# A two-block network on one core: elementwise work of GpSimd moved to the vector engine up to the end of the expert loop

## The chip, the core and the metric

The kernel runs on one NeuronCore of a Trainium2 chip. Such a core has a matrix engine (PE in the profile, with its weight loads as PEld), a vector engine (DVE), a scalar engine (ACT), GpSimd (POOL) and SyncE (SP), which issues most of the DMAs. The metric is the device time of one launch in microseconds (us); lower is better. About 0.2% is what repeated timings of this kernel can tell from no change.

## The reference, cut to what matters

512 tokens of width 1024 pass through two blocks.

- First block. 16 meta tokens are put in front. A normalised input times `w_in` gives five parts: a gated convolution of 3 taps, and a gated convolution of 31 taps over 512 channels with a layer norm behind it. Their outputs, normalised, go through `w_out` into the residual. Then comes a layer of 16384 experts: for each token and each of 8 heads the 16 best experts out of 128 x 128 are chosen by two half-keys of 128 (`top_k` of 16 on either half, then `top_k` of 16 over the sums). An expert is one row of `u` and one row of `v`: the output is the sum over the chosen experts of `gelu(u . x) * gate * v`.
- Second block. A gated feed-forward layer of width 2816, two attention mixers with gates, and another such feed-forward layer.

All products must hold nearly float32 precision. The kernel therefore splits each matrix into a high part (a cast to fp32r) and a low part (the float32 value minus the high part) and adds three products: high x high, high x low, low x high.

## The kernel before, in words

**Weights.** `load_w` (line 79) takes a tile of 128 x 1024 float32 weights by DMA into `wf`, then `split` (line 89) casts it to the high part `wh` on the scalar engine (line 93) and subtracts to the low part `wl` (line 98). The low part is made on the vector engine by default and on GpSimd where the caller says `lo="p"`. `wf`, `wh` and `wl` have three buffers each, shared by all callers.

**Order.** Each engine works through its own queue in order. The Tile framework lays out these queues: it follows program order as a priority and its own timeline of when an instruction can start. A few instructions are kept in program order by hand (`keep_in_program_order`): the GpSimd gathers and the first product of each step of the pinned expert tiles.

**First block** (`block1`). 20 column tiles of `w_in` go through `proj` (line 198); their low parts are made on GpSimd, but for the first. `conv` (line 211) makes the 31 taps of one of four channel tiles: a tap is one multiply-add of 128 x 512 on the vector engine (line 221). For channel tile 0, 20 of its taps are instead a scalar-engine multiply (line 218) and a GpSimd addition (line 219). Twelve products with the norm's factor `rs` are on GpSimd too: `sg` (line 239), `xs` (line 274), `cv` (line 289), four each.

**Routing** (`peer`, lines 458 to 536). For each head two tiles of `peer_wq` are multiplied (low parts on GpSimd from head 1 on), scored against the half-keys, and the vector engine picks the best 16 by max, index and replace operations; candidates are built by small additions (line 487) and a GpSimd subtraction `dk` (line 507, which the change leaves alone) serves to read the chosen expert's number. In the shadow of this the matrix engine runs expert tiles 2 to 14 (`u_tile`, line 538), which come later in program order.

**Gate matrix** (lines 542 to 567). Three of the four token tiles go through all experts ("dense"); for them a matrix of gates by expert is needed. For each block of 8 tokens, one-hot rows of the first half-index (`o1`, line 556) and of the second (`oa`, line 557) are made by comparing `iota` with broadcast values, 128 x 1024 at once. `o1` times the gate gives `ob`: 5 of the 8 tokens on GpSimd (line 558), 3 on the scalar engine (line 560). 8 products `oa` x `ob` (line 564, two groups of four) are copied to `stg` by the scalar engine and sent to DRAM for each 16 tokens. Expert tiles 15 to 21 are spread as pinned steps among these blocks.

**Expert loop** (lines 569 to 635). In each of 128 iterations: the activations of a coming expert tile (`u_steps`, line 397: 24 products of 128 x 384, the low part of `u_t` on GpSimd), the gated activation `hf` (line 624) and its split, and 18 products of 128 x 512 with `peer_v` (low part on the vector engine; on GpSimd in the last 25 iterations, which have no `u` tile). The fourth token tile takes its experts by gathers instead: 256 indirect DMAs issued by GpSimd (lines 576 and 587), each followed by a multiply-add over 128 x 1024 on the vector engine (lines 579 and 590); four `row` buffers.

**Behind it** come the second block's feed-forward and attention, with some elementwise work on GpSimd that the change doesn't touch.

Of the kernel before, what the change touches and what calls it, by code (L numbers as in the profile page):

```python
# [27 lines left out]
# columns of the packed per-channel vectors, [128, NCONST]  # L28
# [17 lines left out]
class Ctx:  # L46
    def split_x(self, n=T):
        """The two parts of what the next products take, [128, 8, n]."""
        self.hh = self.xp.tile([P, KD, NM + T], F32R, tag="hh", name="hh", bufs=1)[:, :, 0:n]
        self.hl = self.xp.tile([P, KD, NM + T], F32R, tag="hl", name="hl", bufs=1)[:, :, 0:n]  # L50
        return self.hh, self.hl

    def split_tok(self):
        """The same, token tile by token tile: [128, 4, 8, 128]."""
        r = []
        for tag in ("hh", "hl"):
            t = self.xp.tile([P, KD, NM + T], F32R, tag=tag, name=tag, bufs=1)
            r.append(t.rearrange("p k n -> p (k n)")[:, 0:KD * T].rearrange("p (t k n) -> p t k n", t=4, k=KD))
        self.hh, self.hl = r
        return r  # L60

    def rows(self):
        """8 tiles [128, T], two to a buffer"""
# [15 lines left out]
def load_w(c, src, lo="v", hi="a", n=1024, p=P):  # L79
    """One weight unit [128, n]: the float32 values and their exact two-part split."""  # L80
# [20 lines left out]
def tok_ss(c, pool, tp, srcs, width):  # L101
    """PSUM [128, tiles]: sums of squares over the channels, token on the partitions.

    srcs: the channel tiles [128 channels, width]."""
# [15 lines left out]
def rsqrt(c, out, ss, n):  # L120
    """out = 1 / sqrt(ss / n + eps), a few columns; one Newton step on the table's square root

    Several n are those of as many parts of the columns."""
# [16 lines left out]
def col_rs(c, pool, tp, srcs, n, width, tag, bufs=1):  # L140
    """PSUM [128, width]: 1 / sqrt(mean over the n channels + eps) of each column, on every partition."""
# [16 lines left out]
def block1(c, A):  # L158
# [7 lines left out]
    with ExitStack() as es:  # L166
# [23 lines left out]
        # the products take the residual times the gain; the norm's factor of a token goes to what they give  # L190
# [7 lines left out]
        def proj(j, w=None):  # L198
            wh, wl = w or load_w(c, A["w_in"][j], lo="p")
# [11 lines left out]
        def conv(i, pool_taps=()):  # L211
            """A channel tile of the 31 taps, a step for each tap."""
            o = CONST_COLS["cf_w"][0] + 31 * i
            nc.scalar.activation(out=acc[i], in_=ub[:, i, 0:T], func=AF.Identity, scale=C[:, o:o + 1], bias=col("cf_b", i))
            for k in range(1, 31):
                if k in pool_taps:
                    t = tp.tile([P, T], F32, tag="tap", name="tap", bufs=2)
                    nc.scalar.mul(out=t, in_=ub[:, i, k:k + T], mul=C[:, o + k:o + k + 1])
                    nc.gpsimd.tensor_tensor(out=acc[i], in0=acc[i], in1=t, op=ALU.add)
                else:  # L220
                    nc.vector.scalar_tensor_tensor(out=acc[i], in0=ub[:, i, k:k + T], scalar=C[:, o + k:o + k + 1], in1=acc[i], op0=ALU.mult, op1=ALU.add)
# [12 lines left out]
        for i in range(4):  # L234
# [4 lines left out]
            nc.gpsimd.tensor_tensor(out=sg, in0=sg, in1=rs, op=ALU.mult)  # L239
# [3 lines left out]
            if i == 0:  # L243
                taps = conv(0, range(31 - c.ptaps, 31))
                some_taps(30 - c.ptaps)
# [4 lines left out]
        def gained(src, gname, i, k, l):  # L250
            """A channel tile times the gain, in two parts; its squares."""
# [18 lines left out]
        for i in range(4):  # L270
# [3 lines left out]
            nc.gpsimd.tensor_tensor(out=xs, in0=xs, in1=rs, op=ALU.mult)  # L274
# [14 lines left out]
            nc.gpsimd.tensor_tensor(out=cv, in0=cv, in1=rs[:, NM:], op=ALU.mult)  # L289
# [55 lines left out]
        # the next norm, token on the partitions; then features on the partitions, split  # L345
# [27 lines left out]
        # the first of the experts' tiles need the dense tokens only  # L373
# [8 lines left out]
GT = 3            # the token tile whose experts are gathered; the others go through all experts  # L382
ND = 3 * P        # tokens of the dense tiles
# [6 lines left out]
GRP = 8           # expert tiles whose gates are read at once  # L390
TG = 16           # tokens per block of the gate matrix


def u_steps(c, A, i, ps, alloc, pin=False):
    """The activations of 128 experts for the dense tokens, a step for each k-tile; pinned, a step stays behind
    what is before it on the tensor engine."""
    nc = c.nc
    wh, wl = load_w(c, A["u_t"][i], lo="p")
# [15 lines left out]
def peer(c, A):  # L414
# [9 lines left out]
    with ExitStack() as es:  # L424
# [26 lines left out]
        with tc.tile_pool(name="pr", bufs=1) as pr, tc.tile_pool(name="prp", bufs=2, space=PSUM) as pp:  # L451
# [6 lines left out]
            # routing, head by head  # L458
            mxs = []
            for h in range(NH):  # L460
                VI = pr.tile([P, 2, 2, 4, TOPK], F32, tag="VI", name="VI", bufs=2)
                ii = pr.tile([P, 2, 4, TOPK], U32, tag="ii", name="ii", bufs=2)
                for half in range(2):
                    wh, wl = load_w(c, A["peer_wq"][2 * h + half], lo="p" if h else "v")
# [36 lines left out]
                # the chosen experts: candidate j's key is j * 2^15 + expert - 2^14; less position * 2^15,  # L501
                # the chosen one's is the only one of an absolute value up to 2^14 that stands for an expert
# [8 lines left out]
            # gates: softmax over the chosen 16 of each head  # L511
# [10 lines left out]
            # the dense tiles' experts and gates, slot on the partitions  # L522
# [19 lines left out]
        with tc.tile_pool(name="pg", bufs=1) as pg, tc.tile_pool(name="pgp", bufs=2, space=PSUM) as pp:  # L542
            B, BP = 8, 5
            for tg in range(ND // TG):
                stg = pg.tile([P, NE, TG], F32, tag="stg", name="stg", bufs=2)
                for q in range(TG // B):
# [7 lines left out]
                    o1 = pg.tile([P, B, P], F32, tag="o1", name="o1", bufs=2)  # L554
                    ob = pg.tile([P, B, P], F32, tag="ob", name="ob", bufs=3)
                    nc.vector.tensor_tensor(out=o1, in0=ib, in1=both(0), op=ALU.is_equal)  # L556
                    nc.vector.tensor_tensor(out=oa, in0=ib, in1=both(1), op=ALU.is_equal)  # L557
                    nc.gpsimd.tensor_tensor(out=ob[:, 0:BP, :], in0=o1[:, 0:BP, :], in1=both(2)[:, 0:BP, :], op=ALU.mult)
                    for j in range(BP, B):
                        nc.scalar.activation(out=ob[:, j, :], in_=o1[:, j, :], func=AF.Copy, scale=sT[:, 2, t0 + j:t0 + j + 1])  # L560
# [10 lines left out]
        with tc.tile_pool(name="pd", bufs=1) as pd, tc.tile_pool(name="pv", bufs=1, space=PSUM) as pv:  # L571
# [33 lines left out]
            def gathers(spent):  # L605
                """Spread over the time of the loop: an iteration without a U or V tile is half as long."""
# [9 lines left out]
            for i in range(NE):  # L616
# [11 lines left out]
                wh, wl = load_w(c, A["peer_v"][i * P:(i + 1) * P, :], lo="v" if i + LAG < NE else "p")  # L628
# [5 lines left out]
            # the residual; then features on the partitions, with the gains, not yet scaled by the norms  # L634
# [35 lines left out]
def to_split(c, k, g):  # L670
    """Feature tile k of the residual times the gain, not yet scaled by the norm, in two parts."""
# [17 lines left out]
def spread(c, pool, tp, r, tag):  # L689
    """PSUM [128, T]: r, [128, 4] with the token on the partitions, on every partition."""  # L690
# [9 lines left out]
def norm_scale(c, pool, tp, sstag, tag, first=None):  # L700
    """The norm's factors of the tokens, [128, 4] with the token on the partitions and [128, T]."""
# [13 lines left out]
def ffn(c, A, pfx, out=None, then=None):  # L715
    """Expects hh + hl = the residual times the gain; the norm's factor of a token goes to the products."""
# [54 lines left out]
MH = 8            # heads of each mixer  # L771
# [5 lines left out]
PI2_1 = 6.28125                     # 2 pi in three parts; products with small integers are exact  # L777
# [5 lines left out]
def rope_tables(c, A, pool, tp):  # L783
    """cos and sin of position * frequency, [128 tokens, tile, 16]"""
# [27 lines left out]
def rotate(eng, out, x, cos, sin, tmp, n):  # L812
    """out[..., 0:16], out[..., 16:32] = rotary of x; all [128, n, .]"""
# [8 lines left out]
def attention(c, A):  # L822
# [9 lines left out]
    with ExitStack() as es:  # L832
# [10 lines left out]
        fkT = at.tile([P, MH, T], F32, tag="fkT", name="fkT")     # the other head's rows of a pair are zero  # L843
# [15 lines left out]
        # the output gates, before their sigmoid  # L859
# [14 lines left out]
        with tc.tile_pool(name="pre", bufs=1) as lq, tc.tile_pool(name="pret", bufs=2) as tp:  # L874
# [8 lines left out]
            def tokmajor(w, n, evac):  # L883
                """evac(tile, PSUM [128 tokens, n]) of h @ w"""
# [17 lines left out]
            # latents  # L902
# [4 lines left out]
            # fox: q, k normalized per head; then features on the partitions, with the gains  # L907
# [28 lines left out]
            # latents normalized; then features on the partitions, with the gains, split  # L936
# [25 lines left out]
            # the shared rotary key  # L962
# [317 lines left out]
```

## Time and profile before

| what | value |
|---|---|
| timed runs, us | 2864.33, 2865.02, 2869.08 (median 2865.02) |
| profiled execution, span from first to last instruction, us | 2862.9 |
| PE busy | 2660.2 us, 93% |
| DVE busy | 1890.5 us, 66% |
| ACT busy | 1035.9 us, 36% |
| POOL busy | 1214.2 us, 42% |
| granted PE clock, mean | 0.969 |

The page gives no time of the profiled execution apart from its span; the span is 2.1 us under the median of the timed runs, so what lies around it is taken as that. By lines of the code the stages lie about so: first block to 235 us, routing to 479, gate matrix to 652, expert loop to 1700, then the second block. A busy share is one of the whole span; a stage's limit has to be read from that stage. In the views by group a row is a set of like instructions with its count, the busy time, the mean duration of one, and the idle time of the engine in front of it with what ended that.

### The profile page before, as it was taken

The numbers are of one execution on the slowest core, as the hardware profiler recorded it, in microseconds if no ns is written. First come the engines' busy times: TensorE is split into PE (matmuls) and PEld (weight loads), VectorE is DVE, ScalarE is ACT, GpSimd is POOL, SyncE is SP. The second block draws the span as 40 slices with busy tenths as digits, with TensorE's granted clock in tenths as the row PEclk, the third lists the DMA queues.
The fourth block names the chain that finished last, engine by engine and source line by source line (L and its number), as shares of the span: only waits on it lengthen the run. The fifth ranks groups of instructions, "written<-read, shape, count | busy, mean of one in ns | idle before, by whom it ended". The sixth has DMA issues, their size and how long they took to land.

```text
span 2862.9 us, 35289 instructions
## 1 busy us (share of the span) xinstructions
PE 2660.2 (93%) x13149; PEld 2272.9 (79%) x13149; DVE 1890.5 (66%) x3126; ACT 1035.9 (36%) x1606; POOL 1214.2 (42%) x725
## 2 busy tenths in 40 slices
PE   7689886779999999999999999999999999999999
PEld 7677775768888888888888777888888787788887
DVE  7985999995778767677777965343344677443322
ACT  4233223874333323333333343222234455332221
POOL 5622555675666666666666842110000222111100
PEclk9799988999999999999999999999999999999999
DMA  4122212448888878878888732223333222323232
GB/s 158 52 74 83 82 60 79 164 171 285 284 287 289 280 270 268 284 266 284 273 277 279 259 118 89 92 92 92 94 109 101 91 72 86 100 92 96 96 99 78
DMA packets 171052, 458.28 MB, mean 160 GB/s; under 512 B 15032, under 2 KB 64568, under 8 KB 167680
## 3 DMA queue, kind: packets, MB, share of 16 engines
q1 hardware_dynamic: 133728, 321.61, 33.7%
q0 software_dynamic: 36864, 134.23, 13.7%
q8 instruction: 103, 1.69, 0.2%
q14 instruction: 69, 0.57, 0.1%
q10 hardware_dynamic: 288, 0.18, 0.0%
HBM read 424.50 MB, written 31.47 MB: 159 GB/s over the span
## 4 chain that ended last, share of the span: by engine, by line
PE 63%; DVE 13%; DMA 8%; issue 4%; POOL 1%; ACT 1%; SPq 0%; POOLq 0%; DVEq 0%; ACTq 0%
PE mm L74 6%; PE mm L76 6%; PE mm L75 6%; PE v L75 4%; DMA wf<-peer_v 4%; PE v L76 4%; PE v L74 4%; PE u L406 3%; PE u L405 3%; PE u L402 3%; PE dn L75 3%; PE dn L76 3%; PE dn L74 3%; DVE o L556 2%; DVE oa L557 2%
## 5 line engine op out<-in xcount | busy, mean ns | idle before, releaser
L93 ACT CAST wh<-wf 128x1024 fp32r<-128x1024 f32 (+2 forms) x487 | 504.9, 1039 | 1128.7 <-PE mm L75 319.0
L98 POOL TENSOR_TENSOR wl<-wf,wh 128x1024 fp32r<-128x1024 f32 x186 | 487.2, 2622 | 412.0 <-ACT wh L93 368.8
L98 DVE TENSOR_TENSOR wl<-wf,wh 128x1024 fp32r<-128x1024 f32 (+2 forms) x301 | 375.0, 1247 | 312.7 <-ACT wh L93 305.1
L406 PE MATMUL u<-hh,wl 128*128 128x384 f32 x1008 | 343.8, 341 | 14.9 <-POOL wl L98 14.9
L402 PE MATMUL u<-hh,wh 128*128 128x384 f32 x1008 | 347.5, 345 | 4.2 <-ACT wh L93 2.5
L405 PE MATMUL u<-hl,wh 128*128 128x384 f32 x1008 | 344.0, 341 | 0.0
L75 PE MATMUL v<-wl,hh 128*128 128x512 f32 x768 | 310.2, 404 | 15.9 <-DVE wl L98 14.0
L74 PE MATMUL v<-wh,hh 128*128 128x512 f32 x768 | 307.2, 403 | 16.0 <-ACT wh L93 16.0
L76 PE MATMUL v<-wh,hl 128*128 128x512 f32 x768 | 308.2, 401 | 2.5 <-DVE hl L98 2.5
L74 PE MATMUL mm<-hh,wh 128*128 128x512 f32 x704 | 278.9, 397 | 5.7 <-ACT hh L674 3.5
L76 PE MATMUL mm<-hh,wl 128*128 128x512 f32 x704 | 279.2, 397 | 0.0
L75 PE MATMUL mm<-hl,wh 128*128 128x512 f32 x704 | 278.9, 396 | 0.0
L590 DVE SCALAR_TENSOR_TENSOR h_tok<-row,gwt,h_tok 128x1024 f32<-128x1024 f32 x128 | 227.2, 1775 | 56.6 <-DMA row<-peer_v,gidx 56.1
L579 DVE SCALAR_TENSOR_TENSOR jkd<-row,xg 128x1024 bf16<-128x1024 f32 x128 | 215.2, 1681 | 60.5 <-DMA row<-peer_u,gidx 60.1
L747 POOL TENSOR_TENSOR sg<-sg,rs 128x512 f32<-128x512 f32 x44 | 75.8, 1725 | 391.4 <-ACT sg L746 391.4
L406 PEld LDWEIGHTS u<-hh,wl 128*128 128x128 f32 x1008 | 192.9, 191 | 16.4 <-POOL wl L98 16.4
L402 PEld LDWEIGHTS u<-hh,wh 128*128 128x128 f32 x1008 | 193.3, 192 | 9.6 <-ACT wh L93 3.0
L405 PEld LDWEIGHTS u<-hl,wh 128*128 128x128 f32 x1008 | 193.2, 192 | 4.8
L576 POOL DMA_INDIRECT row<-peer_u,gidx x128 | 177.3, 1385 | 37.5 <-issue 19.9
L587 POOL DMA_INDIRECT row<-peer_v,gidx x128 | 178.9, 1398 | 30.5 <-issue 21.5
L75 PEld LDWEIGHTS v<-wl,hh 128*128 128x128 f32 x768 | 147.1, 192 | 54.0 <-DVE wl L98 20.6
L74 PEld LDWEIGHTS v<-wh,hh 128*128 128x128 f32 x768 | 147.0, 191 | 50.3 <-ACT wh L93 19.3
(377 smaller groups left out, 5386.9 us busy)
## 6 DMA issues: line engine op xcount, KB each, us to landing
wf<-u_t SPq DMA_DIRECT2D x128, 512.0 KB
wf<-peer_v SPq DMA_DIRECT2D x128, 512.0 KB
gates_d<-stg SPq DMA_DIRECT2D x24, 1024.0 KB
gt<-gates_d SPq DMA_DIRECT2D x16, 1536.0 KB
wf<-f_g SPq DMA_DIRECT2D x44, 512.0 KB
wf<-f_u SPq DMA_DIRECT2D x44, 512.0 KB
wf<-f_d SPq DMA_DIRECT2D x32, 512.0 KB
wf<-w_in SPq DMA_DIRECT2D x20, 512.0 KB
```

Source lines behind the costliest of these rows:

```text
L74: nc.tensor.matmul(ps, lh, rh, start=start, stop=False)
L75: nc.tensor.matmul(ps, lh, rl, start=False, stop=False)
L76: nc.tensor.matmul(ps, ll, rh, start=False, stop=stop)
L93: nc.scalar.copy(out=h, in_=f)
L98: (nc.vector if lo == "v" else nc.gpsimd).tensor_tensor(out=l, in0=f, in1=h.bitcast(F32), op=ALU.subtract)
L402: mm = nc.tensor.matmul(ps3, lh, rh, start=k == 0, stop=False)
L405: nc.tensor.matmul(ps3, lh, rl, start=False, stop=False)
L406: nc.tensor.matmul(ps3, ll, rh, start=False, stop=k == KD - 1)
L576: dm = nc.gpsimd.indirect_dma_start(out=row, out_offset=None, in_=A["peer_u"], in_offset=bass.IndirectOffsetOnAxis(ap=gidx[:, s:s + 1], ax ...
L579: nc.vector.scalar_tensor_tensor(out=jk, in0=row, scalar=1.0, in1=xg, op0=ALU.mult, op1=ALU.mult, accum_out=gact[:, s:s + 1])
L587: dm = nc.gpsimd.indirect_dma_start(out=row, out_offset=None, in_=A["peer_v"], in_offset=bass.IndirectOffsetOnAxis(ap=gidx[:, s:s + 1], ax ...
L590: nc.vector.scalar_tensor_tensor(out=hh, in0=row, scalar=gwt[:, s:s + 1], in1=hh, op0=ALU.mult, op1=ALU.add)
```

## The change

All elementwise work of GpSimd in the first block, and all of it in the expert layer but the subtraction `dk`, goes to the vector engine. `lo="p"` disappears from every `load_w`: the low parts of `w_in`, `u_t`, `peer_wq` and of the last `peer_v` tiles are now line 98 on the vector engine. The 20 taps become multiply-adds of the vector engine, and their scalar-engine multiplies go. The twelve products `sg`, `xs`, `cv` change engine. In the gate matrix `o1` and both ways of multiplying it vanish; `ob` is made by 8 `tensor_scalar` operations of 128 x 128, one for each token, that compare `iota` with the token's index and multiply by its gate, both given as per-partition scalars. `oa`, the products, the gathers and `dk` stay. The rest of the diff removes comments.

```diff
 def proj(j, w=None):
-    wh, wl = w or load_w(c, A["w_in"][j], lo="p")
+    wh, wl = w or load_w(c, A["w_in"][j])
...
-        def conv(i, pool_taps=()):
+        def conv(i):
...
             for k in range(1, 31):
-                if k in pool_taps:
-                    t = tp.tile([P, T], F32, tag="tap", name="tap", bufs=2)
-                    nc.scalar.mul(out=t, in_=ub[:, i, k:k + T], mul=C[:, o + k:o + k + 1])
-                    nc.gpsimd.tensor_tensor(out=acc[i], in0=acc[i], in1=t, op=ALU.add)
-                else:
-                    nc.vector.scalar_tensor_tensor(out=acc[i], in0=ub[:, i, k:k + T], scalar=C[:, o + k:o + k + 1], in1=acc[i], op0=ALU.mult, op1=ALU.add)
+                nc.vector.scalar_tensor_tensor(out=acc[i], in0=ub[:, i, k:k + T], scalar=C[:, o + k:o + k + 1], in1=acc[i], op0=ALU.mult, op1=ALU.add)
...
-            nc.gpsimd.tensor_tensor(out=sg, in0=sg, in1=rs, op=ALU.mult)
+            nc.vector.tensor_tensor(out=sg, in0=sg, in1=rs, op=ALU.mult)
...
-                taps = conv(0, range(31 - c.ptaps, 31))
-                some_taps(30 - c.ptaps)
+                taps = conv(0)
+                some_taps(10)
...
-            nc.gpsimd.tensor_tensor(out=xs, in0=xs, in1=rs, op=ALU.mult)
+            nc.vector.tensor_tensor(out=xs, in0=xs, in1=rs, op=ALU.mult)
...
-            nc.gpsimd.tensor_tensor(out=cv, in0=cv, in1=rs[:, NM:], op=ALU.mult)
+            nc.vector.tensor_tensor(out=cv, in0=cv, in1=rs[:, NM:], op=ALU.mult)
...
-    wh, wl = load_w(c, A["u_t"][i], lo="p")
+    wh, wl = load_w(c, A["u_t"][i])
...
-                    wh, wl = load_w(c, A["peer_wq"][2 * h + half], lo="p" if h else "v")
+                    wh, wl = load_w(c, A["peer_wq"][2 * h + half])
...
-                    o1 = pg.tile([P, B, P], F32, tag="o1", name="o1", bufs=2)
                     ob = pg.tile([P, B, P], F32, tag="ob", name="ob", bufs=3)
-                    nc.vector.tensor_tensor(out=o1, in0=ib, in1=both(0), op=ALU.is_equal)
                     nc.vector.tensor_tensor(out=oa, in0=ib, in1=both(1), op=ALU.is_equal)
-                    nc.gpsimd.tensor_tensor(out=ob[:, 0:BP, :], in0=o1[:, 0:BP, :], in1=both(2)[:, 0:BP, :], op=ALU.mult)
-                    for j in range(BP, B):
-                        nc.scalar.activation(out=ob[:, j, :], in_=o1[:, j, :], func=AF.Copy, scale=sT[:, 2, t0 + j:t0 + j + 1])
+                    for j in range(B):
+                        t = t0 + j
+                        nc.vector.tensor_scalar(out=ob[:, j, :], in0=iota, scalar1=sT[:, 0, t:t + 1], scalar2=sT[:, 2, t:t + 1], op0=ALU.is_equal, op1=ALU.mult)
...
-                wh, wl = load_w(c, A["peer_v"][i * P:(i + 1) * P, :], lo="v" if i + LAG < NE else "p")
+                wh, wl = load_w(c, A["peer_v"][i * P:(i + 1) * P, :])
```

## Rows read from the trace of the kernel before

**Rows 1.** Busy us (count) of PE, PEld, DVE, ACT, POOL by stage; clock, DMA share, GB/s.
```profile
50.00:200.00 150.00, 111.56 (x763) 105.74 (x762) 145.39 (x138) 43.81 (x58) 87.38 (x43) 0.86 0.20 64
...
300.00:479.00 179.00, 136.85 (x663) 121.37 (x662) 174.31 (x760) 40.02 (x53) 104.28 (x55) 0.90 0.22 74
479.00:652.00 173.00, 129.89 (x900) 117.62 (x899) 171.01 (x98) 137.48 (x250) 119.58 (x54) 0.92 0.40 157
652.00:1700.00 1048.00, 1009.23 (x4904) 890.83 (x4903) 778.46 (x759) 347.33 (x489) 695.66 (x385) 0.98 0.80 270
```

**Rows 2.** VectorE in time order, expert loop at 861: start, duration, instruction.
```profile
861.84 2.65 DVE L624 TENSOR_TENSOR hf<-act,gt 128x384 f32<-128x384 f32 x1
...
865.67 1.23 DVE L579 SCALAR_TENSOR_TENSOR jkd<-row,xg 128x1024 bf16<-128x1024 f32 x1
```

**Rows 3.** GpSimd in time order, the same stretch.
```profile
861.65 2.43 POOL L98 TENSOR_TENSOR wl<-wf,wh 128x1024 fp32r<-128x1024 f32 x1 [7.11 <-ACT wh L93]
...
865.90 1.80 POOL L576 DMA_INDIRECT row<-peer_u,gidx  x1 [0.59 <-DVE jkd L579]
```

**Rows 4.** Line 98, the whole span: count, shortest/median/longest ns.
```profile
L98 DVE TENSOR_TENSOR wl<-wf,wh x301: 898/1224/3420, 5.6 to 2844.2; 128x1024 fp32r<-128x1024 f32 x140, 128x768 fp32r<-128x768 f32 x9, 128x720 fp32r<-128x720 f32 x2
...
L98 DVE TENSOR_TENSOR hl<-hf,hh x128: 542/548/2770, 671.9 to 1686.1; 128x384 fp32r<-128x384 f32 x128
```

**Rows 5.** Groups of instructions, 50 to 200 us: busy us, mean ns, idle before.
```profile
L221 DVE SCALAR_TENSOR_TENSOR rows<-up,cst,rows 128x512 f32<-128x512 f32 x90 | 110.8, 1276 | 0.4
...
L98 POOL TENSOR_TENSOR wl<-wf,wh 128x1024 fp32r<-128x1024 f32 x13 | 35.9, 2760 | 19.8 <-ACT wh L93 19.7
L219 POOL TENSOR_TENSOR rows<-rows,tap 128x512 f32<-128x512 f32 x20 | 33.9, 1697 | 7.3 <-ACT tap L218 3.6 <-DVE rows L221 3.5
```

**Rows 6.** The tap line, the whole span: count, shortest/median/longest ns.
```profile
L221 DVE SCALAR_TENSOR_TENSOR rows<-up,cst,rows x100: 733/744/2892, 36.0 to 183.5; 128x512 f32<-128x512 f32 x100
```

**Rows 7.** Groups of the vector engine, 300 to 479 us.
```profile
L487 DVE TENSOR_TENSOR CE<-VI 128x16 f32<-128x16 f32 (+5 forms) x56 | 39.1, 762 | 0.0
...
L489 DVE TENSOR_TENSOR CE<-VI 128x64 f32<-128x64 f32 x7 | 1.5, 210 | 0.0
```

**Rows 8.** Groups of GpSimd, 240 to 479 us.
```profile
L98 POOL TENSOR_TENSOR wl<-wf,wh 128x1024 fp32r<-128x1024 f32 x31 | 75.2, 2438 | 61.7 <-ACT wh L93 58.5 <-PE sc L472 3.2
```

**Rows 9.** Groups of instructions, 479 to 652 us (gate matrix).
```profile
L558 POOL TENSOR_TENSOR ob<-o,sT 128x640 f32<-128x640 f32 x48 | 101.3, 2113 | 56.3 <-DVE o L556 28.2 <-PE g L564 28.1
L556 DVE TENSOR_TENSOR o<-iota,sT 128x1024 f32<-128x1024 f32 x48 | 99.3, 2074 | 2.2 <-PE trs L534 2.2
...
L557 DVE TENSOR_TENSOR oa<-iota,sT 128x1024 f32<-128x1024 f32 x48 | 77.3, 1616 | 0.0
...
L98 POOL TENSOR_TENSOR wl<-wf,wh 128x1024 fp32r<-128x1024 f32 x5 | 16.7, 3343 | 0.0
```

**Rows 10.** The nearest operation to the new one, `dg`, in time order at 204 us.
```profile
204.18 0.88 DVE L153 TENSOR_SCALAR dg<-ident,rt 128x128 f32<-128x128 f32 x4
```

**Rows 11.** The same operation, the whole span: count, shortest/median/longest ns.
```profile
L153 DVE TENSOR_SCALAR dg<-ident,rt x9: 221/278/288, 25.7 to 204.8; 128x128 f32<-128x128 f32 x8, 16x16 f32<-16x16 f32 x1
```

**Rows 12.** Groups of the vector engine, 652 to 1700 us (expert loop).
```profile
L590 DVE SCALAR_TENSOR_TENSOR h_tok<-row,gwt,h_tok 128x1024 f32<-128x1024 f32 x128 | 227.2, 1775 | 56.6 <-DMA row<-peer_v,gidx 56.1
L579 DVE SCALAR_TENSOR_TENSOR jkd<-row,xg 128x1024 bf16<-128x1024 f32 x127 | 214.0, 1685 | 60.5 <-DMA row<-peer_u,gidx 60.1
...
L98 DVE TENSOR_TENSOR hl<-hf,hh 128x384 fp32r<-128x384 f32 x128 | 116.0, 907 | 17.3 <-ACT hh L93 17.2
L624 DVE TENSOR_TENSOR hf<-act,gt 128x384 f32<-128x384 f32 x128 | 110.1, 862 | 5.3 <-DMA gt<-gates_d 3.4
```

**Rows 13.** Groups of GpSimd, the same stretch.
```profile
L98 POOL TENSOR_TENSOR wl<-wf,wh 128x1024 fp32r<-128x1024 f32 x130 | 341.4, 2627 | 274.6 <-ACT wh L93 234.7 <-issue 38.0 <-PE g L564 1.5
```

**Rows 14.** Waits of the matrix engine, 652 to 1700 us: total, times, longest.
```profile
PE v L74 <- ACT wh L93: 16.0, 8, 3.7
PE v L75 <- DVE wl L98: 14.0, 14, 2.4
```

More of the change, by code (lines that the diff above doesn't have):

```diff
@@ L542, in peer @@
         with tc.tile_pool(name="pg", bufs=1) as pg, tc.tile_pool(name="pgp", bufs=2, space=PSUM) as pp:
-            B, BP = 8, 5
+            B = 8
             for tg in range(ND // TG):
@@ L1169, in emit @@
     c.first, c.act = 2, {}
-    c.ptaps = 20
     c.lag, c.inside, c.early = 25, 7, 3
```

## The prediction

> **What bounds the kernel now.** I read the profile's stages first, then the groups inside each stage, then the longest and shortest duration of single lines. Stages [rows 1]: in the convolutions of the first block (50 to 200 us) the vector engine is busy 145.4 of 150 us, in the routing 174.3 of 179, in the gate matrix 171.0 of 173. In all three it is the bound, with the matrix engine under 77% busy. In the expert loop the matrix engine is the bound, 1009 of 1048 us, and the vector engine has 270 us free. The second block isn't touched.
>
> At first sight, then, the change loads the one engine that is full. The single durations say something else. A product `hf` of 128x384 takes 2.65 us where GpSimd runs a low part from 861.65 to 864.08, and ends 0.4 us after it [rows 2, 3]; the like-sized `hl` takes 0.55 at the median and up to 2.77 [rows 4]. A tap takes 0.744 at the median, 1.276 on the mean of the full stretch and 2.89 at worst [rows 5, 6]. In the gate matrix both compares are 128x1024, yet one averages 2.07 and the other 1.62 [rows 9], against 1.22 for the same number of elements of `wl` on the same engine [rows 4]. So much of the vector engine's busy time is time in which a two-input operation stands still until GpSimd's elementwise instruction ends. An indirect DMA on GpSimd doesn't do this: `jkd` takes 1.23 beside one of 1.80 us [rows 2, 3]. What I weigh is therefore, in each stage, blocked time given back against work taken over. Operations of the vector engine follow each other with 0.08 us of overlap (four `dg` of 0.28 in 0.88 us, so one each 0.20 [rows 10, 11]); I take this off each added one.
>
> **First block.** Given back: 90 taps by 1.276 - 0.744 = 47.9 us [rows 5, 6]. Added in that stretch: 20 taps by 0.67 = 13.4; 13 low parts by 1.22 - 0.08 = 1.14 [rows 4, 5] = 14.8; ten products `sg`, `xs`, `cv` at no more than a tap's 0.67 = 6.7; sum 34.9. Net -13. The blocked time of smaller groups is not counted, so it may be -20; if a quarter of the returned time is lost to waits for the shorter chains, 0. The matrix engine is not late here: 111.6 of 150 us busy.
>
> **Routing.** Here most vector work is max, index and replace on one source, and the added low parts come on top: 31 by 1.14 = 35.3 us [rows 4, 8]. Given back: the candidate additions, 56 by 0.762 - 0.21 = 30.9, the smallest of six forms costing 0.21 with the overlap or less [rows 7]; part of that belongs to `dk`, which stays on GpSimd, and other small groups add to it. I take 27. Net +8; bounds 0 and +35 (nothing comes back).
>
> **Gate matrix.** 48 blocks [rows 9]. Gone: `o1`, 48 x (2.074 - 0.08) = 95.7 us. `oa` falls from 1.616 to 1.22: 48 x 0.40 = 19.0. Added: 5 low parts by 1.14 = 5.7, and 384 `tensor_scalar` of 128x128. None like it with two scalars and two operations is in the trace. The nearest is `dg`, same shape, one scalar: one each 0.20 us [rows 10, 11]. Below, the 16x16 form takes 0.221 in all, 0.14 with the overlap [rows 11]; above, 0.34 if the second scalar costs 0.06 and nothing overlaps (a tap, with one scalar, takes 0.744 [rows 6], and 0.06 is my estimate from it against the 0.68 that 512 elements would take on the line through 0.548 for 384 and 1.22 for 1024 [rows 4]). I take 0.23, near `dg` with half the second scalar: 384 x 0.23 = 88.3. Net -95.7 - 19.0 + 5.7 + 88.3 = -21, so 171 becomes 150. At 0.20 it is -32, at 0.34 +22; at 0.14 the vector engine would need 115 us and the matrix engine's 129.9 busy us [rows 1] would take over, -41. The scalar engine loses its 144 multiplies and isn't late.
>
> [...]
>
> **Expert loop.** Given back: 128 x (1.775 - 1.23) + 127 x (1.685 - 1.23) + 128 x (0.907 - 0.548) + 128 x (0.862 - 0.548) = 69.8 + 57.8 + 46.0 + 40.2 = 214 us [rows 2, 4, 12]. Added: 130 by 1.14 = 148 [rows 13]. So the vector engine falls from 778 to about 712 of 1048; hidden behind the matrix engine, this is worth nothing by itself. What counts is the matrix engine's waits [rows 14]: 14.0 us in 14 pieces for low parts, of which I count 10 as blocked by GpSimd; and 16.0 us in 8 pieces for high parts, whose weights landed late. A weight buffer is reloaded when its low part is done, and that comes 2.63 - 1.22 = 1.4 us sooner for a `u` tile [rows 4, 13]; 8 x 1.4 = 11, of which half. Together -16; bounds 0 and -30 (all of the 30.0 us). The three DMAs and queues that matter (SP's weight loads, GpSimd's gathers) keep their order; GpSimd is left with the gathers alone, which can then go as soon as a `row` buffer is free.
>
> **Sum.** -13 + 8 - 21 - 16 = -42. The profiled execution's span is 2862.9 and the median of the timed runs lies 2.1 above it: 2865.0 - 42 = 2823.
>
> **Rivals.**
>
> (a) More comes back. First block -20, routing 0, gate matrix -32, loop -30: -82, 2783. For it: the uncounted small groups. Against: late weights have other causes than the buffer.
>
> (b) The low parts queue badly. The expert tiles that run in the shadow of the routing get their low parts from GpSimd's empty queue. On the full vector engine they have the lowest priority, since they come last in the program. If they starve until the routing is over, 13 tiles x 24 products at 1048/4904 = 0.214 us [rows 1] = 67 us of matrix work stand alone in front of the gate matrix, and the routing gets 13 x 1.14 = 15 back: -42 + 67 - 15 = +10, 2875. It decides from the point where more than 10 of the 13 slip; at five, the time is -22. For it: 174.3 of 179 us busy [rows 1]. Against: time returned in front of it, and any gap lets one through.
>
> (c) The one-hot is dear, 0.34 us each: -42 + 43 = +1, 2866. Then the changed kernel isn't different. For it: two scalars, never seen here. Against: `dg`.
>
> (d) The gathers hurt. The vector engine, in order, already stands 56.1 + 60.1 us for `row` [rows 12], and now every `u` low part queues behind these waits too. If half of that reaches the matrix engine and the loop's gain is lost: -42 + 16 + 58 = +32, 2897. For it: GpSimd's issue beside a busy vector engine takes 1.80 us [rows 3]. Against: low parts of `peer_v` are in the same queue today and cost 14.0 us in all [rows 14]. [...]
>
> **How the numbers follow.** The sum 0.54, own range 2800 to 2850; (a) 0.16; (b) 0.14; (c) 0.09; (d) 0.07. A difference under 0.2%, 5.7 us, can't be told from none. Faster takes the sum, (a) and a part of (b) where few tiles slip: 0.72. Same takes most of (c): 0.08. Slower takes most of (b), the rest of (c), and (d): 0.20. The range goes from (a) to past (b): 2782 to 2880.
>
> **What would show it.** Taps at 0.74 throughout; `hf` and `hl` near 0.55 on the mean; the mean of `oa` at 1.22; the new line at 0.25 to 0.3 us, one each 0.23; a gate stage near 150 us; the loop near 1032. Wrong would be: stages that stay as long with the vector engine's idle time grown (rival b: expert tiles 2 to 14 behind the routing; rival d: waits of the matrix engine for low parts over 30 us in the loop), or a one-hot over 0.3 us each.

## The result, and the profile after

The changed kernel takes 2770.56 us (median of 4 runs, 2769.51 to 2775.14) against 2866.7 beside it: a ratio of 0.9662, 95% interval 0.9633 to 0.9692, or 96 us less. The forecast was 2823 us, its range 2782 to 2880. The sign was right; the gain is more than twice the forecast one, and the time lies 11 us below the range.

The stages, cut in both traces at the same products of the matrix engine (first `q`, first and last `g`, first `mm`, end), in us:

| | first block | routing | gate matrix | expert loop | second block |
|---|---|---|---|---|---|
| before | 261.9 | 221.0 | 170.4 | 1052.0 | 1157.6 |
| after | 238.8 | 217.0 | 155.0 | 1003.6 | 1159.0 |
| difference | -23.1 | -4.0 | -15.4 | -48.4 | +1.4 |
| forecast | -13 | +8 | -21 | -16 | 0 |

The stages of the changed kernel, columns as in [rows 1]:

```profile
36.00:155.00 119.00, 108.43 (x869) 106.30 (x867) 117.97 (x168) 31.32 (x37) 0.00 (x0) 0.97 0.28 89
...
240.00:449.00 209.00, 168.75 (x826) 147.26 (x824) 193.73 (x943) 45.79 (x60) 55.19 (x33) 0.89 0.22 74
...
611.00:1614.00 1003.00, 991.34 (x4906) 882.85 (x4904) 722.62 (x900) 353.67 (x497) 351.14 (x253) 1.00 0.81 283
```

The vector engine (third of the busy times) still fills the early stages, but is quicker through them; in the loop it has less to do than before, 722.6 against 778.5 us, with 130 low parts more. Its groups there answer to [rows 12] and [rows 14]:

```profile
L583 DVE SCALAR_TENSOR_TENSOR h_tok<-row,gwt,h_tok 128x1024 f32<-128x1024 f32 x128 | 164.1, 1282 | 15.2 <-DMA row<-peer_v,gidx 14.0 <-DVE hl L98 0.3
L572 DVE SCALAR_TENSOR_TENSOR jkd<-row,xg 128x1024 bf16<-128x1024 f32 x127 | 155.3, 1223 | 7.4 <-DMA row<-peer_u,gidx 6.3
L98 DVE TENSOR_TENSOR hl<-hf,hh 128x384 fp32r<-128x384 f32 x128 | 71.2, 557 | 122.7 <-ACT hh L93 121.6 <-PE v L76 1.1
L617 DVE TENSOR_TENSOR hf<-act,gt 128x384 f32<-128x384 f32 x128 | 71.1, 556 | 7.4 <-DMA gt<-gates_d 5.2
```
```profile
PE v L74 <- ACT wh L93: 4.1, 3, 2.0
PE u L397 <- ACT wh L93: 2.4, 1, 2.4
PE tr L645 <- DVE h_tok L654: 1.6, 1, 1.6
PE u L401 <- DVE wl L98: 1.2, 2, 0.6
PE v L74 <- ACT hh L93: 0.3, 1, 0.3
```

`hf` and `hl` have come to 0.56 us, and the multiply-adds to 1.22 and 1.28: their means lie at the lengths that the kernel before had where GpSimd left them alone. The waits for `row` went from 116.2 to 20.3 us. And the matrix engine's waits for low parts of `peer_v`, 14.0 us before, are gone.

### The profile page after: what moved, and what is told of

It reads as the page before. It is cut to its first block, busy times and chain, and to the rows that moved or that the text cites. A ratio compares the mean times of both kernels' runs of the same rounds, so it can differ in the third digit from the quotient of the medians.

```text
span 2773.4 us, 35271 instructions
## 1 busy us (share of the span) xinstructions
PE 2635.6 (95%) x13149; PEld 2252.9 (81%) x13149; DVE 1792.5 (65%) x3680; ACT 991.1 (36%) x1442; POOL 576.9 (21%) x459
## 4 chain that ended last, share of the span: by engine, by line
PE 67%; DVE 13%; DMA 7%; issue 2%; POOL 1%; ACT 1%; POOLq 0%; DVEq 0%; ACTq 0%; SPq 0%
PE mm L74 6%; PE mm L76 6%; PE mm L75 6%; PE v L74 5%; PE v L75 5%; PE v L76 5%; PE u L401 4%; PE u L400 3%; PE u L397 3%; DVE ob L553 3%; PE dn L76 3%; PE dn L74 3%; PE dn L75 3%; DMA wf<-peer_v 2%; DVE oa L550 2%
## 5 line engine op out<-in xcount | busy, mean ns | idle before, releaser
L98 DVE TENSOR_TENSOR wl<-wf,wh 128x1024 fp32r<-128x1024 f32 (+2 forms) x487 | 594.8, 1224 | 334.4 <-ACT wh L93 328.8
L75 PE MATMUL v<-wl,hh 128*128 128x512 f32 x768 | 303.9, 396 | 0.0
L74 PE MATMUL v<-wh,hh 128*128 128x512 f32 x768 | 291.8, 396 | 4.4 <-ACT wh L93 4.1
L569 POOL DMA_INDIRECT row<-peer_u,gidx x128 | 171.4, 1339 | 364.1 <-DVE jkd L572 335.3
L93 ACT CAST hh<-hf 128x384 fp32r<-128x384 f32 x128 | 65.7, 513 | 309.7 <-PE v L75 250.6
L583 DVE SCALAR_TENSOR_TENSOR h_tok<-row,gwt,h_tok 128x1024 f32<-128x1024 f32 x128 | 164.1, 1282 | 15.2 <-DMA row<-peer_v,gidx 14.0
L76 PEld LDWEIGHTS v<-wh,hl 128*128 128x128 f32 x768 | 144.2, 188 | 34.9 <-DVE hl L98 0.3
L74 PEld LDWEIGHTS mm<-hh,wh 128*128 128x128 f32 x704 | 133.4, 190 | 37.3 <-DVE rows L647 2.7
```

Source lines behind the costliest of these rows:

```text
L74: nc.tensor.matmul(ps, lh, rh, start=start, stop=False)
L75: nc.tensor.matmul(ps, lh, rl, start=False, stop=False)
L76: nc.tensor.matmul(ps, ll, rh, start=False, stop=stop)
L93: nc.scalar.copy(out=h, in_=f)
L98: (nc.vector if lo == "v" else nc.gpsimd).tensor_tensor(out=l, in0=f, in1=h.bitcast(F32), op=ALU.subtract)
L569: dm = nc.gpsimd.indirect_dma_start(out=row, out_offset=None, in_=A["peer_u"], in_offset=bass.IndirectOffsetOnAxis(ap=gidx[:, s:s + 1], ax ...
```

## The experiments

Ratios are to the kernel before, timed beside each; stage lengths are cut as above, from the one profiled execution of each run.

### The loop by itself (e1) and all but the loop (e2)

```diff
 # e1, in the kernel before                          # e2, in the changed kernel: the same two lines reversed
-    wh, wl = load_w(c, A["u_t"][i], lo="p")
+    wh, wl = load_w(c, A["u_t"][i], lo="p" if i < c.lag - c.early else "v")
-                ... lo="v" if i + LAG < NE else "p")
+                ... lo="v")
```

> The kernel before, with only the expert loop's low parts (u tiles from number 22 on, and the last 25 peer_v tiles) on the vector engine. Theory: in the loop GpSimd's subtraction holds up two-input vector operations, and with them the low and high parts that the matrix engine waits for; the loop alone then gives back about what it did in the whole change, 48 us of 1052, so 2818 to 2825, and hf and hl fall to 0.55 us each. Rival (the stages are coupled: the loop became shorter because earlier stages left its gathers and weights in another phase): under 25 us, over 2840.

Measured: 2823.17, ratio 0.9832 (0.9799 to 0.9866), as the theory had it; the loop takes 1005.0 us.

> The changed kernel, with the loop's low parts (the same tiles as in e1) back on GpSimd. Theory: the three earlier stages keep their 42 us (first block 23, routing 4, gate matrix 15), the loop is back at 1045 to 1055 us: 2815 to 2825. Rival (coupling): the loop stays near 1005 to 1030 and the time under 2800.

Measured: 2832.3, ratio 0.9871 (0.9833 to 0.9909); the loop takes 1058.2 us, and the early stages keep nearly what the change gave them (238.4, 215.2, 159.2). Time and loop lie 7 and 3 us above the theory's bands, far from the rival's. The two parts, 47 and 38 us, make 85 of the 96; what is missing lies within the intervals. So the stages are nearly separate: about half of the gain belongs to the loop's low parts alone. With them on GpSimd both waits of [rows 14] are back:

```profile
PE v L75 <- DVE wl L98: 17.8, 18, 3.0
PE v L74 <- ACT wh L93: 16.4, 8, 3.8
```

### What a GpSimd operation does to the loop (e3 to e6)

All four start from the changed kernel and add GpSimd work that no result depends on.

```diff
 # e3 (in each loop iteration)
+  scr = pd.tile([P, D], F32, tag="scr", name="scr", bufs=1)
+  nc.gpsimd.tensor_tensor(out=scr, in0=xg, in1=hf[:, 0:1].to_broadcast([P, D]), op=ALU.subtract)
 # e4
+  nc.gpsimd.memset(scr, 0.0)          # scr here 128x2048
+  nc.scalar.activation(out=tin, in_=scr[:, 0:1], func=AF.Copy, scale=hf[:, 0:1])
 # e5 (in u_steps, for the loop's u tiles)
+  nc.gpsimd.tensor_tensor(out=tie, in0=wh.bitcast(F32)[:, 0:1], in1=c.ones[:, 0:1], op=ALU.subtract)
 # e6 (in each loop iteration)
+  tc.keep_in_program_order(nc.gpsimd.tensor_tensor(out=scr, in0=xg, in1=xg, op=ALU.subtract))
```

> The changed kernel, with one useless GpSimd subtraction of 128x1024 (it reads two SBUF tiles, nobody reads its result) in each of the 128 loop iterations. Theory (two-input vector operations stand still while GpSimd reads SBUF): hf, hl and the gathers' multiply-adds grow again on the mean by some 0.2 to 0.4 us, and the loop loses 10 to 45 us although no weight depends on GpSimd: 2781 to 2816. Rival (what counted was the 1.2 us shorter way of the u low part itself and the sooner free weight buffer): no more than 5 us, 2766 to 2776.

> As e3, but GpSimd fills 128x2048 with zero in each iteration (about as long, reads nothing; a tiny scalar-engine operation ties it to the iteration). Theory (only a GpSimd operation that reads SBUF holds the vector engine): vector operations keep their lengths and the time stays within 5 us of the changed kernel, 2766 to 2776. Rival (GpSimd's being busy delays the gathers, and that was the loss): as long as e3, 2781 to 2816.

> The changed kernel, with one tiny GpSimd operation (128x1) for each u tile of the loop, which reads one column of that tile's high part: GpSimd's queue waits in order for the weights, as it did before the change, but does next to nothing. Theory A (the loop's 48 us came from vector operations no longer standing still behind GpSimd's subtractions): the loop stays at 1003 to 1012 us, 2766 to 2780. Theory B (they came from the gathers, which no longer stand behind those waits in GpSimd's queue; late gathers hold up the vector queue and with it the low parts): the vector engine waits over 100 us for row, the loop takes 1030 to 1060, 2797 to 2830.

> As e3 (a useless GpSimd subtraction of 128x1024 for each loop iteration), but it reads a constant tile alone, so it waits for nothing, only its place among the gathers. Theory A: hf, hl and the multiply-adds grow by some 0.1 to 0.4 us on the mean, and the loop loses 20 us or more: over 2790. Theory B: the gathers still run ahead, the vector engine waits little for row, the loop loses under 12 us: 2768 to 2784.

| | time, us | ratio (interval) | loop, us |
|---|---|---|---|
| changed | 2770.56 | 0.9662 (0.9633 to 0.9692) | 1003.6 |
| e3 pass tied to `hf` | 2939.15 | 1.0236 (1.0201 to 1.0270) | 1164.7 |
| e4 memset tied to `hf` | 2862.97 | 0.9968 (0.9953 to 0.9982) | 1093.8 |
| e5 tie only | 2801.97 | 0.9765 (0.9743 to 0.9788) | 1026.1 |
| e6 pass, untied | 2877.79 | 1.0036 (1.0019 to 1.0053) | 1112.6 |

The times of e3 and e4 are outside what any theory had foreseen. e6 came out as its theory A, with a loss far over the 20 us that it asked for; e5 as its theory B, with a loop 4 us shorter than its band. Vector groups of e6 in its loop, then its matrix engine's waits:

```profile
L98 DVE TENSOR_TENSOR wl<-wf,wh 128x1024 fp32r<-128x1024 f32 x238 | 358.6, 1509 | 88.7 <-ACT wh L93 88.4
L583 DVE SCALAR_TENSOR_TENSOR h_tok<-row,gwt,h_tok 128x1024 f32<-128x1024 f32 x128 | 211.4, 1651 | 1.4 <-DMA row<-peer_v,gidx 0.5
...
L617 DVE TENSOR_TENSOR hf<-act,gt 128x384 f32<-128x384 f32 x128 | 108.7, 850 | 6.3 <-DMA gt<-gates_d 4.5
```
```profile
PE u L401 <- DVE wl L98: 55.7, 38, 3.7
PE v L75 <- DVE wl L98: 18.4, 14, 5.4
```

Here the subtraction needs no result of the loop and the gathers are in time (0.5 us of waiting for `row`), yet `hf` is back at 0.85 and low parts take 1.51 us; the loop loses 109. That is the standing still, by itself. In the trace, the 20 `hf` that start while a subtraction runs take 2.24 us at the median and end 0.42 us after it. Then e4, in the same order:

```profile
L583 DVE SCALAR_TENSOR_TENSOR h_tok<-row,gwt,h_tok 128x1024 f32<-128x1024 f32 x128 | 164.2, 1283 | 179.6 <-DMA row<-peer_v,gidx 179.4
L572 DVE SCALAR_TENSOR_TENSOR jkd<-row,xg 128x1024 bf16<-128x1024 f32 x127 | 155.1, 1222 | 103.6 <-DMA row<-peer_u,gidx 102.7
L617 DVE TENSOR_TENSOR hf<-act,gt 128x384 f32<-128x384 f32 x128 | 70.9, 555 | 8.8 <-DMA gt<-gates_d 4.6 <-ACT tin L623 2.3
```
```profile
PE u L401 <- DVE wl L98: 45.9, 31, 4.2
PE v L75 <- DVE wl L98: 20.5, 20, 3.0
```

No vector group is longer than in the changed kernel, and the 12 `hf` that start while a fill runs take 0.56 us at most: these fills, which read nothing, didn't hold the engine up. But the vector engine stands 282 us for `row`, since the gathers now wait in GpSimd's queue for the loop's pace, and the low parts stand behind those multiply-adds. The scalar engine, too, now stands 410 us for `hf` before its tiny operation, with casts behind it; how much of the 90 us comes from that was not tested. e5 leaves the scalar engine out and shows that the gathers' waiting costs time with an operation of nearly no length:

```profile
DVE jkd L575 <- DMA row<-peer_u,gidx: 127.1, 63, 7.6
DVE h_tok L586 <- DMA row<-peer_v,gidx: 115.0, 64, 6.3
```
```profile
PE u L404 <- DVE wl L98: 17.0, 12, 3.9
```

It costs 22.5 us of the loop (31 us between the medians of the timed runs). e3 has both, 261 us of waits for `row` and the longer vector operations, and loses 161. So both ways of losing time are real in the changed kernel, whose two low parts share one vector queue. They need not have been what the kernel before lost by: there the `u` low part was not in that queue.

### Weight buffers in the kernel before (e9, e13, e14)

```diff
-def load_w(c, src, lo="v", hi="a", n=1024, p=P):
+def load_w(c, src, lo="v", hi="a", n=1024, p=P, own=None):
-    wf = c.wst.tile([P, n], F32, tag="wf", name="wf", bufs=c.nwf)
+    wf = (own or c.wst).tile(...)        # own: a tag of its own, 2 buffers
-                ... lo="v" if i + LAG < NE else "p")
+                ... lo="v" if i + LAG < NE else "p", own=pd)
 # e13: in the loop 1 buffer for u_t and 2 for peer_v;  e14: 2 and 1
```

> The kernel before, with two weight buffers of their own for peer_v, so that its loads no longer wait until a u tile's low part is done on GpSimd. Theory (the 16 us for late high parts in the loop before came from weight buffers that were freed late, as the prediction had it): the matrix engine's waits for high parts fall from 18.5 to under 8 us, its half-clock time falls with them, the loop loses 10 to 25 us: 2840 to 2857. Rival (they come from the DMA traffic itself, whose gathers and gate reads the weights share): waits and time as before, 2860 to 2872.

Measured: 2817.46, ratio 0.9822 (0.9801 to 0.9842), 23 us below the expected band; the loop takes 1007.5 us. GpSimd still makes its low parts there and still stretches the vector engine, and that engine still waits 144 us for `row`:

```profile
L101 DVE TENSOR_TENSOR hl<-hf,hh 128x384 fp32r<-128x384 f32 x128 | 130.6, 1021 | 36.4 <-ACT hh L96 35.3 <-PE v L76 1.1
L627 DVE TENSOR_TENSOR hf<-act,gt 128x384 f32<-128x384 f32 x128 | 114.4, 895 | 5.3 <-DMA gt<-gates_d 3.4
```
```profile
PE v L74 <- ACT wh L96: 7.6, 1, 7.6
PE v L76 <- DVE hl L101: 2.2, 3, 1.1
PE v L75 <- DVE wl L101: 1.9, 3, 0.7
```

Yet the loop is 44.5 us shorter, of the 48.4 that the change gave. What the loop lost before was lost where weights came too late, not on the vector engine's own time. The waits for low parts went with it, from 14.0 to 1.9 us, though GpSimd still stretches the vector engine.

The traces also show which loads came late. SyncE issues its loads in order, among them, for every eight tiles, the read of their gates (line 621). Its queue before tile 45 in the kernel before (start, duration, instruction), then in e9:

```profile
1056.32 0.38 SPq L621 DMA_DIRECT2D gt<-gates_d  x1
1056.79 7.34 SPq L83 DMA_DIRECT2D wf<-peer_v  x1
1064.23 0.39 SPq L83 DMA_DIRECT2D wf<-u_t  x1
```
```profile
1035.31 0.38 SPq L624 DMA_DIRECT2D gt<-gates_d  x1
1035.78 7.08 SPq L86 DMA_DIRECT2D wf<-u_t  x1
1042.96 0.62 SPq L86 DMA_DIRECT2D wfv<-peer_v  x1
```

The issue of a load right behind a gate read lasts 3 to 12 us in these traces, that of the other `peer_v` loads 0.3 us at the median. In the kernel before, 14 of the 16 loads in that place are of `peer_v`; of the first 100 tiles, such a load goes out 8.2 us before its first product (median), the others 16.0. All eight waits for a high part of `peer_v` [rows 14] are for such loads. In e9 and in the changed kernel only 2 and 7 of the 16 are of `peer_v`; in e2, with the waits back, 14 again. So what the change and the two buffers brought is also another order in SyncE's queue. No run changes that order alone.

> The kernel before, with three weight buffers in the loop as before, but one kept for u and two for peer_v. If e9's 45 us came from peer_v's loads no longer waiting for GpSimd's low part of a u tile, with the number of buffers beside the point: loop 1005 to 1020 us, time 2815 to 2832, the matrix engine's waits for high parts of peer_v under 8 us. If e9's gain came from five buffers in place of three: the loop stays at 1045 or more (one buffer for u is scarcer still), 2855 or more.

> The same with two buffers for u and one for peer_v. If only the order of release counts: as e13. If the depth for peer_v counts (its load of 512 KB must start long before it is used, beside the gathers and the gate reads): loop 1060 us or more, waits for the high parts of peer_v over 25 us, 2865 or more.

Measured: e13 2942.94, ratio 1.0261 (1.0239 to 1.0284), loop 1136.8; e14 2966.28, ratio 1.0342 (1.0320 to 1.0364), loop 1158.1. The kind with one buffer starves. The matrix engine's waits in e13, then in e14:

```profile
PE u L405 <- ACT wh L96: 78.4, 17, 8.3
PE v L74 <- ACT wh L96: 8.5, 4, 7.6
```
```profile
PE v L74 <- ACT wh L96: 83.7, 37, 5.3
...
PE u L405 <- ACT wh L96: 12.0, 3, 5.9
```

Where `peer_v` has two buffers of its own its waits are 8.5 us, near e9's 7.6; but by its time e13 came out as its second reading, that five buffers in place of three made e9's gain, and e14 as the reading that depth counts. One buffer for `u` starves `u`, so neither run tells how much of e9's gain is the order of release and how much the number. Either could lengthen the head start of a load. Nor is it settled how the change's share divides between the `u` low part that frees its buffer sooner and the `peer_v` low part that is no longer stretched.

### First block and gate matrix (e10, e8, e11)

e10 puts the `pool_taps` branch of the kernel before back into the changed `conv`, for taps 11 to 30 of channel tile 0, and nothing else.

> The changed kernel with the 20 taps of channel tile 0 back on the scalar engine and GpSimd, nothing else. Theory: an addition on GpSimd keeps the vector engine standing about 1.0 us (a tap of the kernel before averaged 0.53 over its own 0.744, most of it in the stretch of the GpSimd taps) and saves it 0.67: the first stage grows by 4 to 9 us, 2774 to 2780. Rival (the scalar engine and GpSimd have nothing to do there, so work sent to them is gone): 13 us shorter, 2755 to 2762.

Measured: 2779.3, ratio 0.9683 (0.9664 to 0.9701); the first block 246.5, +7.7 us in the profiled runs, as expected. The groups of 36 to 190 us in e10:

```profile
L221 DVE SCALAR_TENSOR_TENSOR rows<-up,cst,rows 128x512 f32<-128x512 f32 x100 | 87.7, 906 | 1.5 <-ACT rows L214 0.9
...
L219 POOL TENSOR_TENSOR rows<-rows,tap 128x512 f32<-128x512 f32 x20 | 32.2, 1608 | 56.6 <-DVE rows L221 45.0 <-ACT tap L218 10.5
```

In the changed kernel all 120 taps take 84.8 us at 0.749:

```profile
L216 DVE SCALAR_TENSOR_TENSOR rows<-up,cst,rows 128x512 f32<-128x512 f32 x120 | 84.8, 749 | 1.2 <-ACT rows L214 0.9
```

In e10 the remaining 100 take 87.7. Giving 20 away made the rest longer than all had been (0.906 us on the mean).

```diff
 # e8, gate matrix of the changed kernel
+  o1 = pg.tile([P, 2, P], F32, tag="o1", name="o1", bufs=2)
+  nc.vector.tensor_tensor(out=o1, in0=ib[:, 0:2, :], in1=both(0)[:, 6:8, :], op=ALU.is_equal)
+  for j in range(6, 8):
+      nc.scalar.activation(out=ob[:, j, :], in_=o1[:, j - 6, :], func=AF.Copy, scale=sT[:, 2, t0 + j:t0 + j + 1])
-  for j in range(B):
+  for j in range(6):
 # e11: as e8, and in gather_u
+  if s < 4: tc.keep_in_program_order(jm)      # jm: the multiply-add of line 572
```

> The changed kernel with the last two of each eight tokens' ob as before the change made on the scalar engine, from a compare of 128x256 on the vector engine. Theory (the gate matrix is bound by the vector engine, eight tensor_scalar at 0.256 us each): a block goes from 1.14 + 8 x 0.256 = 3.19 to 1.14 + 6 x 0.256 + 0.33 = 3.01 us, 48 x 0.18 = -9: 2760 to 2766. Rival (the scalar engine, 105 us busy in the stage, comes too late with two more operations of 0.39 in each block): the same time or longer.

Measured: 2794.09, ratio 0.9738 (0.9717 to 0.9759), longer than the changed kernel; the gate matrix takes 177.0 us. Vector groups in it, 480 to 630 us:

```profile
L557 DVE TENSOR_SCALAR ob<-iota,sT 128x128 f32<-128x128 f32 x240 | 65.0, 349 | 0.0
...
L576 DVE SCALAR_TENSOR_TENSOR jkd<-row,xg 128x1024 bf16<-128x1024 f32 x20 | 24.2, 1211 | 0.0
```

Twenty gathers' multiply-adds in this stretch, 24 in the whole stage, had moved from the loop into the stage whose bound is the vector engine. The planned order, not the scalar engine, made it longer, as e11 shows.

> e8, with the first four gathers' multiply-adds kept in program order on the vector engine, so that none of them runs inside the gate matrix as 24 of them (1.21 us each) did in e8. Theory: without these 29 us a block takes the 3.01 us that e8 was to show; the gate matrix goes from 155 to 146 to 149 us, 2761 to 2766. Rival (the scalar engine is late as well): no gain over the changed kernel, 2768 or more.

Measured: 2767.89, ratio 0.9650 (0.9631 to 0.9669): gate matrix 150.5 us (-4.5, where -6 to -9 was expected), and a time that can't be told from the changed kernel's, 2 us above the band.

### A shorter version (e7, e12)

```diff
-    c.lag, c.inside, c.early = 25, 7, 3
+    c.lag, c.inside, c.early = 30, 7, 3
```

> The changed kernel with c.lag = 30 in place of 25: five more u tiles before the gate matrix and five fewer in the loop (the buffers are those that o1 left free). In the changed kernel the matrix engine has nothing to do from 422 to 449 us. Theory (the routing is bound by the vector engine, the loop by the matrix engine): five tiles of 24 x 0.173 = 4.15 us leave the loop, -21, and the routing gets at most 5 x 1.14 = 6 longer: 2750 to 2758. Rival (the loop is bound by its weights and gathers): no change, 2766 to 2776.

Measured: 2758.62, ratio 0.9616 (0.9596 to 0.9636). Routing 222.9 (+5.9), loop 982.6 (-21.0): the sizes that were expected, and a median just above the band. The end of the routing in the changed kernel, then in e7:

```profile
400.00:456.00 56.00, 22.94 (x126) 20.74 (x124) 51.48 (x199) 10.49 (x15) 24.42 (x15) 0.73 0.25 82
```
```profile
400.00:461.00 61.00, 44.61 (x242) 41.22 (x241) 56.38 (x199) 18.85 (x26) 25.09 (x15) 0.88 0.35 115
```

The matrix engine fills half of what was idle time. Its granted clock, 0.50 of full speed from 426 to 449 us in the changed kernel, rises with that from 0.73 to 0.88 on the mean of the stretch.

> e7 and e11 together: c.lag = 30 and the last two of eight tokens' ob on the scalar engine, gathers pinned. Theory (different stages, so their gains add up): 2746 to 2754. Rival (the gathers, held back, make the loop longer, or the pinned tiles now bound the gate matrix): 2756 or more.

Measured: 2747.82, ratio 0.9573 (0.9555 to 0.9591). This beats both kernels; its interval lies wholly below the changed kernel's.

## Why the prediction was right and wrong

**Right: the mechanism.** Much of the vector time was time held up by GpSimd's elementwise reads. Taps at 0.749 (1.276 before [rows 5]), `hf` and `hl` at 0.56 (0.862 and 0.907 before [rows 12]), and the early stages shorter though their bound took on work, are as told; e10 (taps back at 0.906) and e6 (`hf` back at 0.85) show it by putting single operations back, and e4 shows that a fill doesn't do it (`hf` at 0.555). Where the subtraction starts first in e6, `hf` ends 0.42 us after it; what in the hardware holds `hf` until then was not shown.

**Wrong: the loop, -16 for -48.** The step of the prediction that failed is "Together -16; bounds 0 and -30 (all of the 30.0 us)". Two things were mis-sized. Waits were counted by half: all of the matrix engine's went from 38.6 to 9.6 us, the late high parts with them (16.0 to 4.1), of whose 11 us the step took only half. And waits cost more than their length. Of the waits before, [rows 14] shows the two largest groups; the others are

```profile
PE u L402 <- ACT wh L93: 2.5, 1, 2.5
PE v L76 <- DVE hl L98: 2.5, 1, 2.5
PE v L75 <- POOL wl L98: 1.9, 1, 1.9
PE u L406 <- POOL wl L98: 1.7, 2, 1.6
```

In the kernel before the matrix engine's granted clock is at half of full speed for 34.1 us of the loop, in seven stretches that begin at the end of such a wait or shortly after (waits ending at 681.1, 1074.1, 1217.0, 1430.6, 1502.3, 1596.2 and 1629.6 us; stretches from 681.3, 1073.9, 1217.2, 1432.3, 1503.9, 1596.1 and 1630.2); after the change it is 4.2 us. Not every wait has such a stretch: none follows the one that ends at 1037.1 (2.4 us long). In the stretch from 1596.1 a product of 128x512 starts every 0.43 us, right behind it every 0.23; so, by estimate, the work of the 30 us that are gone now takes 30 x (1 - 0.23 / 0.43) = 14 us less. 29 + 14 = 43 of the 48. The busy time of the matrix engine says the same: for the same 4900 products it fell by 18 us, from 1009.2 [rows 1] to 991.3. The bound of 30 left the clock out.

**The two causes in that step.** Buffers handed back late, the cause named for the late high parts, is borne out only in part. Two more buffers (e9) give 44.5 us, but the late loads are those behind a gate read. The step took it that the weight loads "keep their order"; against the gate reads that order changed. The cause named for the waits for low parts, blocking by GpSimd, is not borne out: in e9 `hf` still averages 0.895 us and these waits are down to 1.9 us. In the kernel before seven of the 14 come 1.3 us behind a wait for the same tile's high part: the load was late for both. Vector time given back in the loop (778 to 723; "about 712" was told) is not where the gain lies, as the step said: e9 gains its 44.5 us with the vector engine busy for 779.

**First block, -13 for -23.** Only the taps' held-up time was counted. In the traces the groups left out (part of "it may be -20") gave back 11 us more, the largest `cv` (8.5 to 5.3 us in 8 operations, here and below without the overlap with the operation in front) and `total` (9.2 to 6.3 in 10), and the taps with the 20 added ones 6 more than told; the low parts took 9 more, as 22 moved and not 13.

**Routing, +8 for -4.** The candidate additions fell from 0.762 to 0.260 on the mean, near what was told, and the low parts cost what was told. What was mis-sized is the sum of the other small groups: together they gave back some 12 us more, the largest the addition of `candk`, 7.7 to 2.1 us in 8 operations.

```profile
L482 DVE TENSOR_TENSOR CE<-VI 128x128 f32<-128x128 f32 (+3 forms) x64 | 12.4, 260 | 0.0
```

**Gate matrix, -21 for -15.** The new operation, one block at 500 us:

```profile
501.94 1.24 DVE L550 TENSOR_TENSOR oa<-iota,sT 128x1024 f32<-128x1024 f32 x1
...
503.08 2.16 DVE L553 TENSOR_SCALAR ob<-iota,sT 128x128 f32<-128x128 f32 x8
...
505.12 1.25 DVE L550 TENSOR_TENSOR oa<-iota,sT 128x1024 f32<-128x1024 f32 x1
```

From one `oa` to the next 3.18 us; less its 1.14, eight operations take 2.04, so 0.255 each. 0.23 had been taken, between 0.14 and 0.34. 384 x 0.025 = 10 us is more than the 5.6 us by which the stage came out longer than told; 4 us in which the vector engine had stood idle there went as well. The length of one was told wrong, too: 0.381 us at the median, where 0.25 to 0.3 was to show it and over 0.3 to refute it. The step goes by the spacing, and that was near. For the routing and the gate matrix no run put the old work back; these accounts rest on the rows alone.

**The rivals.** (a) "more comes back" was nearest, at 2783, and still too high. (b) didn't come: `u` low parts found their gaps, and the tiles were done at 422 us. (c) no, 0.255. (d) no in the changed kernel, whose waits for `row` fell; but e5 shows that low parts behind late gathers do cost time, 22.5 us of its loop.

## What to carry to other kernels

Before work is given to a second elementwise engine, compare the shortest and the mean duration of the first engine's operations: where they part while the second one runs, as for the taps here (0.733 and 1.276 us [rows 5, 6]), "idle" capacity is paid for by the busy engine. Price a wait of the matrix engine with the stretch at the lower clock that may follow it (seven of them here, 34.1 us), and look for its cause in when a buffer is handed back and in what stands before the load in its queue, since in the loop two more buffers (e9) gave nearly what a change of engine gave (44.5 and 48.4 us). An in-order queue that issues gathers should hold nothing that waits for the loop (e5: 22.5 us).

## What the runs showed of the hardware

A vector `tensor_scalar` of 128x128 with two per-partition scalars lasts 0.381 us (median of 384), but one starts every 0.255; with one scalar and one operation it lasted 0.278, one every 0.20 [rows 10, 11]. Which of the two, the second scalar or the second operation, costs the difference was not tested. Beside a GpSimd fill of 128x2048 (1.82 us) two-input vector operations kept their length (0.555 for `hf`, e4), beside a subtraction that reads 128x1024 they grew (`hf` to 0.850, e6).
